# First embedding's projection ahead of and between the first attention's output projections, its input in tiles of the queries' kind

## The chip, the cores and the metric

One core of a Trainium2 chip runs the whole program. The metric is the device time of one execution in microseconds (us); the median of several runs is compared. TensorE (PE) multiplies, VectorE (DVE) and ScalarE (ACT) work on tiles, GpSimd (POOL) does part of that too, SyncE (SP) issues the DMAs.

## What is computed

A decoder of two layers over S = 256 tokens of width D = 1024. The first layer has differential attention (8 heads, each the difference of two softmaxes), the second latent attention; both go on with a gated feed-forward network and a per-layer embedding. Cut to what matters here:

```python
def diff_attention(h, pos, w_qkv, q_gain, k_gain, ...):
    q, k, v = ...                          # rms_norm(h @ w_qkv), per head
    a = softmax(causal(q @ k * scale + bias))
    wts = a[:, :, 0] - lam * a[:, :, 1]
    o = rms_norm(wts @ v, sub_gain) * (1.0 - lam_init)
    return o @ w_o

def per_layer_embedding(h, p_i, norm_g, w_proj, w_gate):
    gate = sigmoid(rms_norm(h, norm_g) @ w_gate)
    return (p_i @ w_proj) * gate

for i in range(2):
    h = h + attention_i(rms_norm(h, attn_norm[i]))
    h = h + conv_gated_ffn(rms_norm(h, ffn_norm[i]), ...)
    h = h + per_layer_embedding(h, p[i], ...)
```

The product `p_i @ w_proj` depends on no activation. It can be computed at any time before the embedding of its layer.

## The kernel before

Every float32 product is made of three faster ones: each operand is split into a high and a low part (`split`, L204 without and L205/L206 with a scale: ScalarE writes the high part, VectorE the difference), and `mm3` (L196 to L200) issues high x high, high x low and low x high into one PSUM tile. Activations lie transposed, features on the partitions.

Weights are streamed: `fetch` (L225) issues one DMA per unit of 128 x 1024 (512 KB) on SP's queue into a ring of five buffers (tile `st`), and `split_unit` has ScalarE cast it (L243, tile `wh`) and VectorE or POOL subtract (L244, tile `wl`), in turn by a share; there are four such pairs. The projection's two units of an embedding have a pair ring of their own (`xh`, `xl`), and their subtraction is always POOL's. A layout table (`_layout`, L1273) puts the units into memory in the order in which they are fetched.

In the first layer two streams of work are woven together (`weave`, L160). The main stream is the heads: `s1` makes a head's scores (tile `pb`; bias added at L554, exponentials at L558, reciprocals at L562/L563, and the combination of the two softmaxes, L565 on ScalarE and L566 on VectorE, tile `ex`); `s2` transposes that combination (tile `pc`) and splits it (`dr`); `s3` multiplies with the values (`pc`) and normalises (square L344, mean L350, a power on POOL L277, scaling L358, tile `da`); `s4` transposes the result and splits it with a gain into `og` (L205, L206). The filler stream `fl_a` (L737) gives the third and fourth projection of queries, keys and values, then the output projection `wo` of heads 0 to 3 and of heads 4 and 5 (tile `pa`, added to the residual at L632), and last the first embedding's input and projection: `pre_load` (L710) with `ple_p` (L703, DMA at L705, tile `d`, split at L204) and `pre_proj` (L717), four groups of twelve matmuls whose results ScalarE copies into `prj` (L732). `pre_proj` yields after each group. Behind the woven part come the output projection of heads 6 and 7, with the residual added in PSUM (L625) and split for the feed-forward (`hgH`, `hgL`), and the feed-forward itself.

A scheduler then sets each engine's order from these two streams and from tile rings: an engine works in that fixed order, and an instruction waits until all that it reads or overwrites is done. PSUM has rings `pa` (3), `pt` (1), `pb` (2) and `pc` (2). In SBUF, tiles of the kind `d` have 7 buffers, `dr` 4, `ex` 4 and `qk` (128 x 2 x 256, queries and keys) 22.

Of the kernel before, what the change touches and what calls it, by code (L numbers as in the profile page):

```python
# [10 lines left out]
F32R = mybir.dt.float32r  # L11
# [83 lines left out]
def trunk(ctx, tc, xT, xN, pT, pos, consts, grow, wall, out):  # L95
# [14 lines left out]
    def bankA():  # L110
        return bank("A")
# [16 lines left out]
    def d_tile(n=512, dt=F32):  # L128
        if dt == F32R:
            return tmp.tile([P, 512], F32R, tag="dr", name="dr", bufs=BUF_DR)[:, :n]  # L130
        return tmp.tile([P, 512], F32, tag="d", name="d", bufs=BUF_D)[:, :n]
# [10 lines left out]
    def f(ap):  # L142
        return ap.bitcast(F32)
# [8 lines left out]
    def later(lag, fn):  # L152
        late.append((clk[0] + lag, fn))
# [48 lines left out]
    def split(hi, lo, src, scale=None):  # L202
        if scale is None:
            return A.copy(hi, src).ins, V.tensor_sub(lo, src, f(hi)).ins  # L204
        return (A.activation(hi, src, AF.Copy, scale=scale).ins,  # L205
                V.scalar_tensor_tensor(lo, src, scale, f(hi), ALU.mult, ALU.subtract).ins)  # L206
# [26 lines left out]
    def ring_pair(tag="w", bufs=BUF_W):  # L233
        return tuple(ring.tile([P, UNIT], F32R, tag=tag + x, name=tag + x, bufs=bufs) for x in "hl")
# [12 lines left out]
    def load_unit():  # L247
        return split_unit(next(fetch()))
# [11 lines left out]
    def col(c, n=1):  # L260
        return cst[:, c:c + n]
# [24 lines left out]
    def qk():  # L286
        return act.tile([P, 2, S], F32R, tag="qk", name="qk", bufs=BUF_QK)
# [46 lines left out]
    def norm_block(ps, nb, width, eps, att=False):  # L334

        parts = [p[:, :nb * width] for p in ps] if isinstance(ps, list) else [ps[:, :NT * nb * width]]
        n, m = NT * nb * width, NT * nb
        s2 = a_tile() if att else d_tile(n)
        sg = "sa" if att else "s"
        ss = small(m, sg)  # L340
        z = n // len(parts)
        if width == P:
            for i in range(m):
                A.activation(s2[:, i * P:(i + 1) * P], ps[:, i * P:(i + 1) * P], AF.Square, accum_out=ss[:, i:i + 1])  # L344
        else:
            for i, p in enumerate(parts):
                A.activation(s2[:, i * z:(i + 1) * z], p, AF.Square)
            nbv[0] = V.tensor_reduce(ss, s2.rearrange("p (a b) -> p a b", b=width), AX.X, ALU.add).ins
        if isinstance(eps, float):
            V.tensor_scalar(ss, ss, 1.0 / width, eps, ALU.mult, ALU.add)  # L350
        else:
            V.scalar_tensor_tensor(ss, ss, 1.0 / width, eps[:, :m], ALU.mult, ALU.add)
        r = small(m, sg)
        rsqrt_(r, ss, m)
        dst = a_tile() if att else d_tile(n)
        w = m // len(parts)
        for i, p in enumerate(parts):
            nbv[1] = V.tensor_mul(dst[:, i * z:(i + 1) * z].rearrange("p (a b) -> p a b", b=width),  # L358
                                  p.rearrange("p (a b) -> p a b", b=width),
                                  r[:, i * w:(i + 1) * w].unsqueeze(2).to_broadcast([P, w, width])).ins  # L360
        return dst

    def to_T(src, dH, dL, gcol, bank=None):

        nb = src.shape[1] // (NT * P)
        pt = (bank or bankT)()
        for t in range(NT):
            for j in range(nb):
                i, o = t * nb + j, j * NT + t
                transpose(pt[:, o * P:(o + 1) * P], src[:, i * P:(i + 1) * P])  # L370
        split(dH.rearrange("p n x -> p (n x)"), dL.rearrange("p n x -> p (n x)"), pt[:, :NT * nb * P], gcol)
# [122 lines left out]
    def proj_a(p):  # L494
        todo = []

        def post(s, ps):
            dH, dL = qk(), qk()
            if s < 2:
                src = norm_block(ps, 4, 64, xs["eps"])  # L500
                if p == 1:
                    bst["after"] = bst.get("after", []) + nbv

                def fin():
                    to_T(src, dH, dL, gq[:, 0:1] if s == 0 else col(C_AK))
                    QA[p]["qk"[s]] = dH, dL
                later(LAG, fin)
            else:
                for t in range(NT):
                    split(dH[:, t], dL[:, t], ps[:, t * S:(t + 1) * S], xs["r"][:, t:t + 1])  # L510
                QA[p]["v"] = dH, dL

        for s in range(3):
            if p == 0 and s == 0:
                ps = first_block()
            else:
                ps = bankA()
                us = [(load_unit(), 4) for i in range(2)]
                block(8, us, S, 0, S, hgH, hgL, ps)
            yield 1  # L520
            todo.append((s, ps))
            if p == 0 and s == 0:
                epsx()
            elif p == 0 and s == 1:
                first_stats()
            elif p == 1 and s == 0:
                bias_prep()
            while "r" in xs and todo:
                post(*todo.pop(0))
# [122 lines left out]
    def wo(h0, kn, post=None):  # L652
        while not done.issuperset(range(h0, h0 + kn)):
            yield None
        yield from wst([(n, k) for n in range(NK) for k in range(kn)], lambda k: oH[(h0 + k) // 4][:, (h0 + k) % 4],
                       lambda k: oL[(h0 + k) // 4][:, (h0 + k) % 4], post)
# [15 lines left out]
    def first_block():  # L672
        ps = [bankA() for _ in range(NT)]
        for k, u, j in get_first():
            for t in range(NT):
                mm3(ps[t][:, :S], hgH[:, k, t * P:(t + 1) * P], hgL[:, k, t * P:(t + 1) * P],
                    u[0][:, j * S:(j + 1) * S], u[1][:, j * S:(j + 1) * S], k == 0, k == NK - 1)
        return ps

    def epsx():  # L680
        V.tensor_scalar(gq[:, 0:1], col(C_AQ), -SCALE_A, None, ALU.mult)
        V.tensor_scalar(gq[:, 1:2], col(C_QN), -SCALE_B, None, ALU.mult)
        V.tensor_scalar(gq[:, 2:3], col(C_ASUB), 1.0 - LAM_INIT, None, ALU.mult)
# [19 lines left out]
    def ple_p(l):  # L703
        pst = d_tile()
        nc.sync.dma_start(pst, pT[l].rearrange("p a b -> p (a b)"))  # L705
        pH, pL = d_tile(512, F32R), d_tile(512, F32R)
        split(pH, pL, pst)
        return pH.rearrange("p (a b) -> p a b", a=2), pL.rearrange("p (a b) -> p a b", a=2)

    def pre_load(l):  # L710

        share[0], was = 1.0, share[0]
        w = {"p": ple_p(l), "w": [split_unit(next(fetch()), ring_pair("x", 2)) for _ in range(2)]}
        share[0] = was
        return w

    def pre_proj(pjw):  # L717

        pH, pL = pjw["p"]
        us = pjw["w"]  # L720
        prj = pjw["y"] = act.tile([P, NK, S], F32, tag="prj", name="prj")
        for i in range(2):
            u = us[i]
            for j in range(2):
                ps = bankA()
                for m in range(2):
                    n = 2 * j + m
                    for k in range(2):
                        b = slice((2 * n + k) * P, (2 * n + k + 1) * P)
                        mm3(ps[:, m * S:(m + 1) * S], u[0][:, b], u[1][:, b], pH[:, k], pL[:, k], k == 0, k == 1)  # L730
                n = 4 * i + 2 * j
                A.copy(prj[:, n:n + 2].rearrange("p a b -> p (a b)"), ps)  # L732
                yield 1.3

    pj = []

    def fl_a():  # L737
        yield from proj_a(2)
        yield from proj_a(3)
        yield from wo(0, 4)  # L740
        yield from wo(4, 2)
        pj.append(pre_load(0))
        yield from pre_proj(pj[0])

    weave(chain(bias_mm(), attn_a()), fl_a(), RATIO_A)


# [484 lines left out]
def _layout(inp, np):  # L1232
    f = lambda n: np.asarray(inp[n], dtype=np.float32)
# [12 lines left out]
    def blocks(lst):  # L1246
        for a in range(0, len(lst), 8):
            units.append(np.concatenate(lst[a:a + 8], axis=1))

    def stationary(w, ks=None):  # L1250
        kt, nt = w.shape[0] // P, w.shape[1] // P
        ks = range(kt) if ks is None else ks
        return [w[k * P:(k + 1) * P, n * P:(n + 1) * P] for n in range(nt) for k in ks]
# [16 lines left out]
    for p in range(4):  # L1270
        for s in range(3):
            natural(wqkv[:, s * 1024 + p * 256:s * 1024 + (p + 1) * 256], 4)
    wo = f("a_w_o")[0]  # L1273
    for a, b in ((0, 4), (4, 6), (6, 8)):
        if a == 6:
            blocks(stationary(f("ple_w_proj")[0]))
        blocks(stationary(wo, range(a, b)))
    ffn(0)
    natural(f("w_dkv"), 3)
# [85 lines left out]
```

## Time and profile before

| | |
|---|---|
| median of 3 runs | 773.33 us (772.85 to 773.79) |
| the profiled execution | 773.53 us, its span 771.7 us |
| granted TensorE clock, mean | 0.998 |
| TensorE busy | 752.7 us, 98% of the span |
| VectorE busy | 571.9 us, 74% |
| ScalarE busy | 484.8 us, 63% |
| GpSimd busy | 257.0 us, 33% |

The span reaches from the first to the last instruction; the profiled execution's own time is 1.8 us longer. The granted clock is a share of TensorE's full speed. A busy time is the time in which at least one instruction of the engine runs; since matmuls overlap, the distance from one start to the next says what a matmul costs.

### The profile page before, as it was taken

How to read it: one execution, taken by the hardware profiler on the slowest of the kernel's cores; microseconds unless marked ns; L12 is line 12 of the kernel's file. 1: busy time of each engine (PE TensorE's matmuls, PEld its weight loads, DVE VectorE, ACT ScalarE, POOL GpSimd, SP SyncE). 2: the span in 40 equal slices, each digit the busy share in tenths (PEclk: the TensorE clock that was granted, in tenths of full speed). 3: DMA queues.
4: the chain of work that ended last, by engine and by line, in shares of the span. 5: the costliest groups of instructions: out<-in, count | busy, mean ns of one | idle time of the engine just before them, and what ended most of it. 6: DMA issues, size and time to landing. Idle time of an engine off the chain costs nothing.

```text
span 771.7 us, 16485 instructions
## 1 busy us (share of the span) xinstructions
PE 752.7 (98%) x6396; PEld 740.2 (96%) x6396; DVE 571.9 (74%) x1147; ACT 484.8 (63%) x1044; POOL 257.0 (33%) x181
## 2 busy tenths in 40 slices
PE   8999999999999999999999999999999999999996
PEld 7999988999999999999889999999999999999996
DVE  6677888668997795548688988776588778875445
ACT  6537777676666665447867876554676666655442
POOL 2664454233333411111414665131342332201230
PEclk9999999999999999999999999999999999999999
DMA  7994344255665576555355133334466566555531
GB/s 283 277 255 153 134 148 143 83 179 181 197 193 179 173 251 203 181 186 166 110 167 183 60 110 111 100 120 139 136 199 187 176 182 193 185 190 177 183 107 56
DMA packets 37519, 127.97 MB, mean 166 GB/s; under 512 B 4672, under 2 KB 6208, under 8 KB 37440
## 3 DMA queue, kind: packets, MB, share of 16 engines
q1 hardware_dynamic: 36432, 126.29, 52.3%
q8 instruction: 50, 0.82, 0.4%
q10 hardware_dynamic: 1008, 0.63, 0.3%
q14 instruction: 29, 0.24, 0.1%
HBM read 125.75 MB, written 1.15 MB: 164 GB/s over the span
## 4 chain that ended last, share of the span: by engine, by line
PE 86%; DVE 5%; ACT 5%; POOL 1%; issue 1%; DMA 1%; ACTq 0%; POOLq 0%
PE pa L198 18%; PE pa L200 18%; PE pa L199 18%; PE pc L200 8%; PE pc L199 8%; PE pc L198 8%; DVE wl L244 2%; ACT wh L243 1%; PE pt L192 1%; PE pb L198 1%; PE pb L199 1%; PE pc L192 1%; PE pb L479 1%; PE pb L200 1%; POOL wl L244 1%
## 5 line engine op out<-in xcount | busy, mean ns | idle before, releaser
L243 ACT CAST wh<-st 128x1024 fp32r<-128x1024 f32 x221 | 231.0, 1050 | 173.1 <-issue 67.9
L244 DVE TENSOR_TENSOR wl<-st,wh 128x1024 fp32r<-128x1024 f32 x166 | 210.8, 1271 | 105.2 <-ACT wh L243 104.9
L244 POOL TENSOR_TENSOR wl<-st,wh 128x1024 fp32r<-128x1024 f32 x55 | 134.8, 2451 | 208.7 <-ACT wh L243 200.2
L200 PE MATMUL pa<-hgH,wl 128*128 128x256 f32 x496 | 141.2, 285 | 0.4 <-POOL wl L244 0.4
L199 PE MATMUL pa<-hgL,wh 128*128 128x256 f32 x496 | 140.3, 283 | 0.0
L198 PE MATMUL pa<-hgH,wh 128*128 128x256 f32 x496 | 140.1, 283 | 0.0
L199 PE MATMUL pa<-og,wh 128*128 128x256 f32 x352 | 99.8, 284 | 0.9 <-DVE og L206 0.9
L301 POOL TENSOR_TENSOR ssq<-ssq,d 128x256 f32<-128x256 f32 x35 | 37.0, 1057 | 191.0 <-ACT d L300 169.3
L198 PE MATMUL pa<-og,wh 128*128 128x256 f32 x352 | 99.8, 286 | 0.3 <-ACT og L205 0.2
L200 PE MATMUL pa<-og,wl 128*128 128x256 f32 x352 | 99.7, 284 | 0.0
L200 PE MATMUL pc<-hgH,wl 128*128 128x256 f32 x336 | 95.4, 284 | 1.0 <-DVE wl L244 1.0
L200 PEld LDWEIGHTS pa<-hgH,wl 128*128 128x128 f32 x496 | 95.2, 192 | 0.7 <-POOL wl L244 0.6
L198 PE MATMUL pc<-hgH,wh 128*128 128x256 f32 x336 | 95.1, 284 | 0.4 <-DVE pa L793 0.4
L198 PEld LDWEIGHTS pa<-hgH,wh 128*128 128x128 f32 x496 | 95.1, 192 | 0.1
L199 PEld LDWEIGHTS pa<-hgL,wh 128*128 128x128 f32 x496 | 95.2, 192 | 0.0
L199 PE MATMUL pc<-hgL,wh 128*128 128x256 f32 x336 | 95.1, 283 | 0.1
L198 PE MATMUL pa<-wh,hgH 128*128 128x256 f32 x320 | 92.5, 294 | 1.5 <-ACT wh L243 0.8
L199 PE MATMUL pa<-wl,hgH 128*128 128x256 f32 x320 | 92.1, 289 | 1.2 <-DVE wl L244 0.6
L200 PE MATMUL pa<-wh,hgL 128*128 128x256 f32 x320 | 91.9, 288 | 0.3 <-DVE hgL L204 0.3
L199 PEld LDWEIGHTS pa<-og,wh 128*128 128x128 f32 x352 | 67.4, 191 | 1.2 <-DVE og L206 1.1
L198 PEld LDWEIGHTS pa<-og,wh 128*128 128x128 f32 x352 | 66.9, 191 | 1.1 <-ACT og L205 0.7
L200 PEld LDWEIGHTS pa<-og,wl 128*128 128x128 f32 x352 | 67.3, 191 | 0.1
(306 smaller groups left out, 1908.0 us busy)
## 6 DMA issues: line engine op xcount, KB each, us to landing
st<-in_wall SPq DMA_DIRECT2D x225, 512.0 KB, 3.6
oh<-s SPq DMA_DIRECT2D x24, 128.0 KB, 6.5
hT<-in_x SPq DMA_DIRECT2D x4, 256.0 KB, 4.9
st<-in_wall SPq DMA_DIRECT2D x4, 256.0 KB, 5.0
st<-in_xn SPq DMA_DIRECT2D x2, 512.0 KB, 7.2
d<-in_p SPq DMA_DIRECT2D x2, 256.0 KB, 3.8
out_h<-hT SPq DMA_DIRECT2D x4, 128.0 KB, 1.9
out_h<-hT ACTq DMA_DIRECT2D x4, 128.0 KB, 1.9
```

Of the source, the lines that this page charges most:

```text
L192: lastmm[0] = T.transpose(o, i, ident).ins
L198: T.matmul(ps, lhsT=aH, rhs=bH, start=start, stop=False)
L199: T.matmul(ps, lhsT=aH, rhs=bL, start=False, stop=False)
L200: lastmm[0] = T.matmul(ps, lhsT=aL, rhs=bH, start=False, stop=stop).ins
L243: A.copy(hi, st)
L244: eng.tensor_sub(lo, st, f(hi))
L301: sqlast[0] = G.tensor_add(sq, sq, t).ins
L479: T.matmul(ps[:, i * 32:(i + 1) * 32], lhsT=lh, rhs=tb[z], start=z == 0, stop=z == 2)
```

## The change

The two tiles of the embedding's input become tiles of the kind `qk` in place of `dr`, in both layers. In the first layer, `pre_load(0)` and the first two groups of the projection are put ahead of the output projection of heads 0 to 3, the other two groups between it and that of heads 4 and 5. The two weight units move ahead of all units of `wo` in the layout, and so in the order of the fetches.

```diff
--- before.py
+++ after.py
@@ -703,9 +703,9 @@
     def ple_p(l):
         pst = d_tile()
         nc.sync.dma_start(pst, pT[l].rearrange("p a b -> p (a b)"))
-        pH, pL = d_tile(512, F32R), d_tile(512, F32R)
-        split(pH, pL, pst)
-        return pH.rearrange("p (a b) -> p a b", a=2), pL.rearrange("p (a b) -> p a b", a=2)
+        pH, pL = qk(), qk()
+        split(pH.rearrange("p a b -> p (a b)"), pL.rearrange("p a b -> p (a b)"), pst)
+        return pH, pL
 
     def pre_load(l):
 
@@ -737,10 +737,13 @@
     def fl_a():
         yield from proj_a(2)
         yield from proj_a(3)
+        pj.append(pre_load(0))
+        ahead = pre_proj(pj[0])
+        yield next(ahead)
+        yield next(ahead)
         yield from wo(0, 4)
+        yield from ahead
         yield from wo(4, 2)
-        pj.append(pre_load(0))
-        yield from pre_proj(pj[0])
 
     weave(chain(bias_mm(), attn_a()), fl_a(), RATIO_A)
 
@@ -1271,9 +1274,8 @@
         for s in range(3):
             natural(wqkv[:, s * 1024 + p * 256:s * 1024 + (p + 1) * 256], 4)
     wo = f("a_w_o")[0]
+    blocks(stationary(f("ple_w_proj")[0]))
     for a, b in ((0, 4), (4, 6), (6, 8)):
-        if a == 6:
-            blocks(stationary(f("ple_w_proj")[0]))
         blocks(stationary(wo, range(a, b)))
     ffn(0)
     natural(f("w_dkv"), 3)
```

What the scheduler makes of it, at three places. The first is TensorE where the heads' stage gives way to the output projections: `pc` from `ex` are the transposes of head 5's combination, `pa` from `og` the output projection, `pa` from `qk` the embedding's projection. Before:

```order
L200 MATMUL pa_1934<-og_1461,wl_1917 128x256
L198 MATMUL pa_1920<-og_1461,wh_1916 128x256 [waits Activation_49]
L198 MATMUL pa_1934<-og_1461,wh_1916 128x256
L192 MATMUL pc_1882<-ident_103,ex_1708 128x128 [waits DVE_49,PE_49]
L192 MATMUL pc_1882<-ident_103,ex_1708 128x128 [waits DVE_49]
L192 MATMUL pc_1882<-ident_103,ex_1708 128x128
L199 MATMUL pa_1920<-og_1462,wh_1916 128x256 [waits DVE_49]
L546 MATMUL pb_1851<-qk_1764,qk_1620 128x128 [waits Activation_49]
L546 MATMUL pb_1852<-qk_1764,qk_1620 128x128 [waits PE_49]
```

The change:

```order
L199 MATMUL pc_1745<-qk_715,dr_1592 128x128
L200 MATMUL pc_1745<-qk_714,dr_1593 128x128
L192 MATMUL pc_1915<-ident_103,ex_1708 128x128 [waits DVE_49]
L198 MATMUL pa_1861<-qk_1844,xh_1850 128x256 [waits PE_49,Activation_49]
L198 MATMUL pa_1947<-qk_1844,xh_1850 128x256
L192 MATMUL pc_1915<-ident_103,ex_1708 128x128 [waits DVE_49]
L192 MATMUL pc_1915<-ident_103,ex_1708 128x128
L199 MATMUL pa_1861<-qk_1845,xh_1850 128x256 [waits DVE_49]
L200 MATMUL pa_1861<-qk_1844,xl_1851 128x256
```

The output projection of heads 0 to 3 left this place: its first matmuls stand behind the projection of `p` now, and the transposes come directly after the nine matmuls of a head's values (`pc` from `qk` and `dr`).

The second place is ScalarE just ahead of that, with the exponentials (L558) and the combination (L565) of head 5. Before:

```order
L558 ACTIVATE ex_1708,sa_1693<-ex_1708,sa_1692 128x128 [waits DVE_49,Activation_49]
L558 ACTIVATE ex_1708,sa_1693<-ex_1708,sa_1692 128x256 [waits DVE_49]
L558 ACTIVATE ex_1713,sa_1693<-ex_1713,sa_1692 128x128 [waits DVE_49]
L558 ACTIVATE ex_1713,sa_1693<-ex_1713,sa_1692 128x256 [waits DVE_49]
L204 CAST dr_1736<-pc_1732 128x384 [waits PE_49]
L565 ACTIVATE ex_1708<-ex_1708,sa_1718 128x128 [waits DVE_49]
L565 ACTIVATE ex_1708<-ex_1708,sa_1718 128x256 [waits Activation_49]
L243 CAST xh_2262<-st_2260 128x1024 [waits DMAHW4_49]
L243 CAST wh_2032<-st_2030 128x1024 [waits DMAHW0_49,PE_49]
L205 ACTIVATE qk_1836<-pa_1775,m_289 128x256 [waits PE_49]
L243 CAST wh_2098<-st_2096 128x1024 [waits DMAHW1_49]
L205 ACTIVATE og_1461<-pc_1740,gq_122 128x256 [waits PE_49]
```

The change:

```order
L558 ACTIVATE ex_1708,sa_1693<-ex_1708,sa_1692 128x128 [waits DVE_49,Activation_49]
L243 CAST wh_2111<-st_2109 128x1024 [waits DMAHW2_49,PE_49]
L558 ACTIVATE ex_1708,sa_1693<-ex_1708,sa_1692 128x256 [waits DVE_49]
L558 ACTIVATE ex_1713,sa_1693<-ex_1713,sa_1692 128x128 [waits DVE_49]
L558 ACTIVATE ex_1713,sa_1693<-ex_1713,sa_1692 128x256 [waits DVE_49]
L204 CAST dr_1736<-pc_1732 128x384 [waits PE_49]
L205 ACTIVATE qk_1836<-pa_1775,m_289 128x256 [waits PE_49]
L243 CAST wh_2169<-st_2167 128x1024 [waits DMAHW3_49]
L205 ACTIVATE og_1461<-pc_1740,gq_122 128x256 [waits PE_49]
L565 ACTIVATE ex_1708<-ex_1708,sa_1718 128x128 [waits DVE_49]
L565 ACTIVATE ex_1708<-ex_1708,sa_1718 128x256 [waits Activation_49]
L204 CAST qk_1844<-d_1842 128x512 [waits DMAHW7_49]
```

One weight cast stands between the exponentials now, the next between `qk` and `og`, and the combination behind both; the weight cast `xh` of the embedding went to an earlier place. POOL's subtraction for `wh_2169` follows two powers (L277) in its order, at the place where it had `xl_2263` and `wl_2099` before.

The third place is ScalarE where the last head's result is made, ahead of the feed-forward (`hgH`). Before:

```order
L243 CAST wh_2466<-st_2464 128x1024 [waits DMAHW2_49,PE_49,Pool_49]
L732 COPY prj_2272<-pa_2273 128x512 [waits DVE_49,PE_49,Activation_49]
L732 COPY prj_2272<-pa_2287 128x512 [waits PE_49]
L205 ACTIVATE og_2023<-pc_2211,gq_122 128x256 [waits PE_49]
L732 COPY prj_2272<-pa_2301 128x512 [waits PE_49]
L732 COPY prj_2272<-pa_2315 128x512 [waits PE_49]
L205 ACTIVATE hgH_2343<-pa_2335,cst_83 128x256 [waits DVE_49]
L205 ACTIVATE hgH_2343<-pa_2348,cst_83 128x256 [waits DVE_49]
```

The change:

```order
L344 ACTIVATE da_2211,sa_2212<-pc_2201 128x128 [waits DVE_49,PE_49,Pool_49]
L344 ACTIVATE da_2211,sa_2212<-pc_2201 128x128
L243 CAST wh_2466<-st_2464 128x1024 [waits DMAHW2_49,PE_49,Pool_49]
L205 ACTIVATE og_2036<-pc_2220,gq_122 128x256 [waits PE_49]
L205 ACTIVATE hgH_2343<-pa_2335,cst_83 128x256 [waits DVE_49,Activation_49]
L205 ACTIVATE hgH_2343<-pa_2348,cst_83 128x256 [waits DVE_49]
L205 ACTIVATE hgH_2343<-pa_2360,cst_83 128x256 [waits DVE_49]
```

The four copies of the projection's results (`prj`), which follow its 48 matmuls on TensorE, stood between the weight cast and `hgH`; they are gone from here. On VectorE the subtraction for `wh_2466` stands directly ahead of the lower half of the same `og` in both.

## Rows read from the trace of the kernel before

**Rows 1.** The page's first part: busy time by engine, share, instructions.

```profile
PE 752.7 (98%) x6396; PEld 740.2 (96%) x6396; DVE 571.9 (74%) x1147; ACT 484.8 (63%) x1044; POOL 257.0 (33%) x181
```

**Rows 2.** Windows: busy us (x instructions) per engine, granted clock, DMA share, GB/s.

```profile
80.00:100.00 20.00, 20.00 (x179) 19.02 (x178) 18.13 (x45) 16.25 (x47) 8.72 (x6) 1.00 0.33 109
100.00:120.00 20.00, 18.03 (x149) 16.56 (x149) 16.86 (x52) 15.73 (x49) 13.12 (x8) 1.00 0.48 159
...
160.00:340.00 180.00, 179.62 (x1500) 179.37 (x1499) 138.86 (x247) 111.45 (x182) 50.92 (x24) 1.00 0.63 196
```

**Rows 3.** Timeline of TensorE: start, duration, engine, line, instruction, [idle before <-releaser].

```profile
106.05 0.28 PE L198 MATMUL pa<-og,wh 128*128 128x256 f32 x1
...
109.03 0.28 PE L200 MATMUL pa<-og,wl 128*128 128x256 f32 x1
109.41 0.51 PE L198 MATMUL pa<-og,wh 128*128 128x256 f32 x2
109.76 0.49 PE L192 MATMUL pc<-ident,ex 128*128 128x128 f32 x3
111.14 0.39 PE L199 MATMUL pa<-og,wh 128*128 128x256 f32 x1 [0.89 <-DVE og L206]
...
116.88 0.62 PE L198 MATMUL pa<-og,wh 128*128 128x256 f32 x3 [0.16 <-ACT og L205]
...
118.10 0.28 PE L200 MATMUL pa<-og,wl 128*128 128x256 f32 x1
119.19 0.30 PE L192 MATMUL pc<-ident,ex 128*128 128x128 f32 x1 [0.82 <-DVE ex L566]
...
128.89 0.28 PE L200 MATMUL pa<-og,wl 128*128 128x256 f32 x1
129.82 0.41 PE L192 MATMUL pc<-ident,da 128*128 128x128 f32 x2 [0.66 <-DVE da L358]
```

**Rows 4.** Timeline of ScalarE, 102 to 108 us.

```profile
102.81 0.40 ACT L558 ACTIVATE ex<-ex,sa 128x128 f32<-128x128 f32 x1 [0.89 <-DVE sa L554]
...
105.70 1.03 ACT L243 CAST xh<-st 128x1024 fp32r<-128x1024 f32 x1
106.64 1.04 ACT L243 CAST wh<-st 128x1024 fp32r<-128x1024 f32 x1
```

**Rows 5.** Timeline of GpSimd, 99 to 104 us.

```profile
99.04 2.39 POOL L244 TENSOR_TENSOR wl<-st,wh 128x1024 fp32r<-128x1024 f32 x1 [2.90 <-ACT wh L243]
101.72 1.81 POOL L277 TENSOR_TENSOR s<-s,neghalf 128x8 f32<-128x8 f32 x1 [0.30 <-DVE s L352]
```

**Rows 6.** The page's DMA issues: count, KB each, median us to landing.

```profile
d<-in_p SPq DMA_DIRECT2D x2, 256.0 KB, 3.8
```

**Rows 7.** Timeline of VectorE, at 99, 102 and 118 us.

```profile
99.31 2.26 DVE L566 SCALAR_TENSOR_TENSOR ex<-ex,sa 128x128 f32<-128x128 f32 x1
...
102.36 0.15 DVE L350 TENSOR_SCALAR sa<-sa 128x2 f32<-128x2 f32 x1
...
118.70 0.35 DVE L566 SCALAR_TENSOR_TENSOR ex<-ex,sa 128x128 f32<-128x128 f32 x1
```

**Rows 8.** Timeline of ScalarE, at 141 us.

```profile
141.03 0.48 ACT L205 ACTIVATE og<-pc,gq 128x256 fp32r<-128x256 f32 x1
```

**Rows 9.** Timeline of VectorE, 138 to 145 us.

```profile
138.53 1.23 DVE L244 TENSOR_TENSOR wl<-st,wh 128x1024 fp32r<-128x1024 f32 x1 [0.25 <-ACT wh L243]
...
144.12 0.43 DVE L625 TENSOR_TENSOR pa<-pa,hT 128x256 f32<-128x256 f32 x1 [2.10 <-PE pa L200]
```

**Rows 10.** Timeline of TensorE, start of the feed-forward stage.

```profile
145.37 0.28 PE L198 MATMUL pc<-hgH,wh 128*128 128x256 f32 x1
145.72 0.39 PE L199 MATMUL pc<-hgL,wh 128*128 128x256 f32 x1
```

**Rows 11.** Timeline of TensorE, in the second layer's attention.

```profile
422.08 0.30 PE L198 MATMUL pb<-qk 128*128 128x128 f32 x1 [1.21 <-DVE s L350]
...
454.99 0.66 PE L192 MATMUL pt<-ident,d 128*128 128x128 f32 x4 [0.65 <-DVE qk L206]
```

## The prediction

> **What bounds the kernel now.** I read the page first: TensorE is busy 752.7 us of the 771.7 [rows 1], so time can only go or come in its gaps. Second, the busy time by window [rows 2]: 20.00 of 20 us at 80 to 100, 179.62 of 180 in the feed-forward stage at 160 to 340, where 1500 matmuls give a pitch of 0.12 us; but only 18.03 of 20 at 100 to 120. The attention heads' stage is where the loss is. Third, TensorE's timeline there [rows 3] names the waits, fourth the timelines of the engines that feed it. Where two rows of [rows 3] are apart by more than their matmuls need, I count the difference as lost. From 109.03 to 111.14 six matmuls (three of them transposes at 0.11) need 0.69 and take 2.11: 1.42 lost, most of it the wait of 0.89 for the second half of a normalised head (og, L206). From 118.10 to 119.19 0.97 is lost on the combination of two softmaxes (ex, L566), from 128.89 to 129.82 0.81, and 0.16 at 116.88. Together 3.4 us. The change can win no more than that here.
>
> **What moves and what doesn't.** The same 48 matmuls (5.8 us at pitch 0.12), two unit casts, two POOL splits, four prj copies and one p transfer are issued as before. The tiles of another kind add no instruction. Prices below come from rows; a step is a row's duration less about 0.1, since each ScalarE row begins that much before the one ahead ends (105.70 + 1.03 against 106.64 in [rows 4]).
>
> **Price 1, earlier weights and p: nothing.** The two projection units now come first of seven on SP's queue, and the other five two places later; their two splits take POOL some 14 us earlier, where TensorE has no gap at all (80 to 100, [rows 2]). Its cover is the matmuls of the fourth projection. Bounds: 0, and 2.4 us if one such split (2.39, [rows 5]) delayed a wait one to one. I take 0: carried into the new order, the split closest to the matmul that needs it still ends some 5 us ahead of it (an estimate). The p transfer stands behind the last of these units on SP and takes 3.8 us [rows 6]. Issued about 103, it lands by 107, while its cast stands on ScalarE behind work that ends at 109.7 (below). Not the bound.
>
> **Price 2, the first hole (about 107.6).** Before, nine matmuls of wo (the output projection) stood among the transposes here. Now TensorE reaches head 5's transposes (pc from ex) sooner: from 106.05 [rows 3] six transposes (0.57) and nine matmuls of 0.112 (1.0) bring it to 107.63. It then needs L566, and the way to it has grown. On ScalarE a weight cast (wh, 1.04) now stands between the first and second exp and waits for a matmul twelve matmuls and three transposes ahead of 106.05, which ends at about 104.55; then three exps, dr and qk (about 0.4 to 0.5 each, [rows 4]) end near 107.7, a second wh (1.04) ends near 108.7, and only then come og and L565, about 109.4. VectorE's L566 is ready at 109.5. But that second wh releases a POOL split at 108.8 that lasts 2.4.
>
> What such a split does is in the trace: L566 at 99.31 took 2.26 and ended with the POOL split of 99.04 + 2.39 = 101.43 [rows 5, 7]; the same instruction took 0.35 at 118.70. So L566 ends at about 111.3, and TensorE has waited 3.7. Two matmuls of the projection then run, and the third waits about 0.3 for p's lower half, whose VectorE step (0.7 as estimate, between 0.48 for 256 columns [rows 8, 9] and twice that) stands behind L566. New waits 4.0 against 3.4 gone: **+0.6**. Everything behind gains 4 us of lead in this stall and 24 matmuls of cover after it, so I let the waits of 119.19 and 129.82 vanish. Bounds: +2.4 if both stay (0.97 + 0.81), -0.5 if L566 isn't held.
>
> The Trainium skill, "SBUF — State Buffer", section "SBUF: two separate sides", says that the port pair shared by VectorE and GpSimd is an exclusive lock, held by whichever instruction started first for its whole length, and that a VectorE instruction with two SBUF inputs wants it against any GpSimd one that reads SBUF. For the splits the trace agrees (2.26 against 0.35 us); it is less clear for POOL's small powers, where L350, with one input, ran in 0.15 at 102.36 inside the 1.81 us power of 101.72 [rows 5, 7]. By the rule the sum is mine; were the lock not there it would be some 1.1 lower, the second rival below.
>
> **Price 3, the cover taken from the tail (137 to 146).** Before, the projection's 48 matmuls stood between the last two heads' output projections and the feed-forward, and head 7's chain (square, mean, power, scale, transpose, og twice) ran beneath them: only 0.23 us is lost, at 145.37 to 145.72 [rows 10]. Now nothing of it is left there. Counted from the end of head 7's values, 24 matmuls of wo cover 2.9 us, and the two transposes and three more matmuls bring TensorE to 3.5. og's upper half (0.48, [rows 8]) ends at 3.8: wait 0.4. Three matmuls later it needs og's lower half; on VectorE a weight split of 1.23 ([rows 9], 138.53), begun at 3.4, stands in front, so that half ends at 5.0: wait 0.85. Six matmuls, then the residual add (0.43), hgH (0.48) and hgL (0.48) follow one after the other with nothing between: waits of 0.7 and 0.45. Sum 2.4, less 0.23: **+2.1**. Bounds: +0.8 (only the three casts that follow each other) and +2.6 (the split begins later).
>
> **Price 4, the second layer: 0.** Its p tiles change ring too, and the order printed for 410 to 545 us shifts by some rows with the same work. The waits there that could go are 1.21 and 0.65 [rows 11]; the same size could come. Bounds -1.9 and +1.9, and I take 0, no row favouring either.
>
> **Sum.** 0.6 + 2.1 = +2.7 on the profiled execution's 773.53, so 776.2; the median of the runs shown, 773.33, is 0.2 lower: **776.0**. What this measurement can tell from no change is 0.2%, 1.55 us.
>
> **Rivals.**
> *Faster: head 5's combination isn't late.* If L566 is done before 107.6, TensorE finds p's projection without a wait and the hole is filled: -3.4 + 2.1 = -1.3, with one of the second layer's two waits gone -1.9 to -2.5: 771 to 772. For it: before, the exps began at 102.81 [rows 4], over 4 us ahead of the hole. Against: the wh now between the exps can't start before 104.55, a second one stands ahead of L565, and ScalarE works in its fixed order, so L565 can't pass them; TensorE would have to be some 2 us earlier at the matmul that frees the first, or 2 us later at the hole for reasons that cost nothing. Decides: L566's end against 107.6. Chance 0.15.
> *The split doesn't hold L566.* Should the POOL split come after L566 (its unit landing over 0.7 us late), L566 is done at 109.9; the wait is 2.3 and p's lower half costs 0.6: 2.9 - 3.4 + 2.1 = +1.6: 774.9, on the edge of same and slower. Against: in the order that fetch waits only for a split of the projections' weights, long done. Chance 0.15, half to each.
> *Given back later.* The second layer's new order loses its two waits: 776.0 - 1.9 = 774.1, no change to tell. For: 1.9 us of waits stand there. Against: nothing in the change aims at them. Chance 0.14.
>
> **How the numbers follow.** Forecast 0.56, its own range 775 to 778. Slower 0.56 + 0.07 = 0.63; same 0.14 + 0.08 = 0.22; faster 0.15. The range runs from 772.8, which leaves out most of the first rival, to 778.0, where the waits of 119.19 and 129.82 stay (776.0 + 1.8 = 777.8).
>
> **What would show it.** Right: in the profile after, one wait of 3 to 4 us near 107.6 on ex L566, an L566 of about 1.8 us that ends with a POOL split, no named wait of more than 0.3 us from 112 to 131, and near 140 three or four waits for og, hgH and hgL of 2 to 2.6 in sum, with 80 to 100 still full. Wrong: no wait at L566 (the first rival), a wait of 2.3 there (the second), waits below 1 us in the tail, or a difference of more than 1 us at 410 to 545. A wait for xl or for p's transfer would show price 1 wrong.

## The result, and the profile after

The change takes 778.17 us, median of 4 runs (776.34 to 778.48), against 773.2 before: a ratio of 1.0064, 95% interval 1.0051 to 1.0076. It is slower, as forecast, by 5.0 us where 2.7 were forecast, and 0.17 us outside the range.

The profiled execution of the change is the shortest of the four: 776.34 us, span 774.6, mean granted clock 0.994 in place of 0.998. Its busy times, the page's first part, answer to [rows 1]:

```profile
PE 753.2 (97%) x6396; PEld 740.8 (96%) x6396; DVE 569.1 (73%) x1147; ACT 485.8 (63%) x1044; POOL 258.4 (33%) x181
```

As much TensorE work as before, in a span that is 2.9 us longer. The windows answer to [rows 2]; the number behind POOL's busy time is the granted clock:

```profile
80.00:100.00 20.00, 20.00 (x178) 19.09 (x178) 16.78 (x45) 16.43 (x47) 13.32 (x8) 1.00 0.56 180
100.00:120.00 20.00, 16.13 (x126) 15.16 (x125) 14.89 (x41) 13.45 (x45) 7.04 (x5) 0.91 0.31 99
...
140.00:160.00 20.00, 17.99 (x131) 16.95 (x130) 13.25 (x28) 12.48 (x32) 4.71 (x7) 0.91 0.25 80
160.00:340.00 180.00, 179.69 (x1499) 179.43 (x1498) 138.75 (x247) 111.92 (x183) 51.90 (x25) 1.00 0.60 194
```

80 to 100 is still full (price 1). The two stretches of the forecast have lost work time, but both also show a clock of 0.91, which no part of the prediction had. TensorE's timeline around the first hole, to be read against [rows 3]:

```profile
106.64 0.28 PE L200 MATMUL pc<-qk,dr 128*128 128x128 f32 x1
110.78 0.47 PE L192 MATMUL pc<-ident,ex 128*128 128x128 f32 x1 [3.87 <-DVE ex L566]
...
112.37 0.42 PE L198 MATMUL pa<-qk,xh 128*128 128x256 f32 x1
112.59 0.41 PE L199 MATMUL pa<-qk,xh 128*128 128x256 f32 x1
...
114.03 0.28 PE L200 MATMUL pa<-qk,xl 128*128 128x256 f32 x1
```

TensorE waits 3.87 us for L566. Behind that, rows of 256 columns are some 0.21 apart (112.37 to 112.59) in place of 0.12, and only from 114.03 on as before. The clock by finer windows, at the hole and at the tail:

```profile
111.00:114.00 3.00, 3.00 (x15) 2.93 (x15) 2.64 (x7) 0.61 (x2) 0.70 (x1) 0.51 0.50 175
114.00:117.00 3.00, 3.00 (x29) 2.53 (x27) 0.15 (x1) 1.17 (x2) 0.00 (x0) 1.00 0.02 5
...
148.00:151.00 3.00, 2.90 (x12) 2.67 (x13) 1.35 (x4) 2.42 (x9) 1.24 (x2) 0.51 0.25 94
```

Where TensorE takes up work after either group of waits, the granted clock is at 0.5, the 1.2 GHz level, for some 3 us. The engines that feed the first hole, first GpSimd, then VectorE, then ScalarE ([rows 4, 5, 7] before):

```profile
108.23 2.35 POOL L244 TENSOR_TENSOR wl<-st,wh 128x1024 fp32r<-128x1024 f32 x1 [3.72 <-ACT wh L243]
```

```profile
108.51 0.48 DVE L206 SCALAR_TENSOR_TENSOR og<-pc,gq,og 128x256 fp32r<-128x256 f32 x1 [0.73 <-ACT og L205]
108.91 2.22 DVE L566 SCALAR_TENSOR_TENSOR ex<-ex,sa 128x128 f32<-128x128 f32 x2
```

```profile
103.62 0.40 ACT L558 ACTIVATE ex<-ex,sa 128x128 f32<-128x128 f32 x1 [1.01 <-DVE sa L554]
...
104.02 1.04 ACT L243 CAST wh<-st 128x1024 fp32r<-128x1024 f32 x1
...
107.06 1.04 ACT L243 CAST wh<-st 128x1024 fp32r<-128x1024 f32 x1
...
108.37 0.80 ACT L565 ACTIVATE ex<-ex,sa 128x128 f32<-128x128 f32 x2
```

It is the chain of price 2: a weight cast between the exponentials (104.02), a second one ahead of L565 (107.06), the POOL split that this releases (108.23, ending at 110.58), and two L566 that together take 2.22 us, which end at 111.13, 0.55 behind the split (rows with x2 stand for both). At the tail:

```profile
144.80 0.28 PE L200 MATMUL pa<-og,wl 128*128 128x256 f32 x1
145.29 0.62 PE L198 MATMUL pa<-og,wh 128*128 128x256 f32 x3 [0.21 <-ACT og L205]
146.51 0.39 PE L199 MATMUL pa<-og,wh 128*128 128x256 f32 x1 [0.60 <-DVE og L206]
...
147.20 0.28 PE L200 MATMUL pa<-og,wl 128*128 128x256 f32 x1
148.10 0.58 PE L198 MATMUL pc<-hgH,wh 128*128 128x256 f32 x1 [0.62 <-ACT hgH L205]
```

From start to start, less the matmuls between (one, three and one at 0.12), 0.37, 0.86 and 0.78 us are lost, for og's upper half, og's lower half and hgH. The next matmul, for hgL, starts 0.52 later, but already under the half clock. In the second layer, of the two waits of [rows 11] the first is still there and the second is gone (two of 0.31 and 0.27 at 393 went too, and one of 0.25 at 436 is new):

```profile
425.69 0.30 PE L198 MATMUL pb<-qk 128*128 128x128 f32 x1 [1.21 <-DVE s L350]
```

For the sums below I cut the time into three stages by the same four TensorE events in every profile: the matmul behind the last of the start's waits for a weight split (about 20 us), the first matmul of the first feed-forward (`pc` from `hgH`), the one (`pb` from `wh` and `og`, about 378) that waits 1.06 us for `og`, and the one of the second layer's end (`pc` from `hgH`, about 574) that waits 0.36 us for its residual. What lies before 20 us has the same order in all kernels but differs from run to run: that event is at 19.98 before, 18.92 in the first profile of the change and 19.79 in the second.

| profile | 20 us to first feed-forward | to 378 | to 574 |
|---|---|---|---|
| before | 125.4 | 232.6 | 195.9 |
| the change | 129.2 | 234.3 | 194.4 |
| the change, second profile | 130.3 | 234.5 | 194.4 |

First stage +3.8 to +4.9, second +1.7 to +1.9, third -1.6. Of the third, the waits just named make 1.0; no row names the rest.

### The profile page after: what moved, and what is told of

Read it like the earlier page. It is cut to its first block, busy times and chain, and to the rows that moved or that the text cites. A ratio compares the mean times of both kernels' runs of the same rounds, so it can differ in the third digit from the quotient of the medians.

```text
span 774.6 us, 16492 instructions
## 1 busy us (share of the span) xinstructions
PE 753.2 (97%) x6396; PEld 740.8 (96%) x6396; DVE 569.1 (73%) x1147; ACT 485.8 (63%) x1044; POOL 258.4 (33%) x181
## 4 chain that ended last, share of the span: by engine, by line
PE 89%; ACT 4%; DVE 4%; issue 1%; POOL 1%; DMA 1%; ACTq 0%; POOLq 0%
PE pa L198 19%; PE pa L199 19%; PE pa L200 19%; PE pc L200 8%; PE pc L199 8%; PE pc L198 8%; ACT wh L243 2%; DVE wl L244 1%; PE pt L192 1%; PE pc L192 1%; PE pb L198 1%; PE pb L199 1%; PE pb L200 1%; PE pb L546 1%; PE pb L479 1%
```

## Experiments

Each run's ratio is to the kernel before, on the same chip. `again`, `kind`, `half_late` and `p_early` stood side by side, then `p_early_half`, `flip`, `busy20` and `kind_qd`, then `busy36` and `place_dr`.

**The change again** (`again`), for a second profile.

> The changed kernel once more, for a second profile. Theory: it is 776.3 to 778.5 again, the wait for L566 in the first hole is 3.5 to 4.2 us, TensorE's granted clock is 0.50 for 3 to 4 us after that hole and again after the waits ahead of the feed-forward, and the first 25 us, whose order is the same as before, differ from the first profile of the change by the 1 us that was gained there by chance. Rival: the clock fall belongs to that one profile; then this one shows 1.00 after both places and is about 3.5 us shorter.

Measured 778.18 us (776.9 to 778.49), ratio 1.0065 (1.0052 to 1.0078). Its windows, behind the first hole and behind the tail's waits:

```profile
112.00:117.00 5.00, 5.00 (x25) 4.93 (x24) 2.53 (x7) 1.08 (x3) 0.70 (x1) 0.50 0.34 105
...
150.00:154.00 4.00, 3.82 (x19) 3.63 (x20) 1.73 (x5) 3.57 (x10) 1.46 (x2) 0.66 0.24 95
```

The wait is 3.87 us again, and both falls of the clock are there; the first is longer here, 0.50 over all of 112 to 117. The rival is out. Of the 1.1 us that the first profile was ahead at 20 us, 0.9 are gone; with the longer half clock that makes the 2.1 us between the two profiled spans (774.6 and 776.7). At the tail the clock fell later here, so the wait for hgL can be read at full clock:

```profile
150.04 0.38 PE L198 MATMUL pc<-hgH,wh 128*128 128x256 f32 x1 [0.62 <-ACT hgH L205]
150.56 0.38 PE L199 MATMUL pc<-hgL,wh 128*128 128x256 f32 x1
```

0.52 from start to start, less one matmul: 0.40 lost, against 0.23 before.

**The tile kind alone** (`kind`), nothing moved:

```diff
-        pH, pL = d_tile(512, F32R), d_tile(512, F32R)
-        split(pH, pL, pst)
-        return pH.rearrange("p (a b) -> p a b", a=2), pL.rearrange("p (a b) -> p a b", a=2)
+        pH, pL = qk(), qk()
+        split(pH.rearrange("p a b -> p (a b)"), pL.rearrange("p a b -> p (a b)"), pst)
+        return pH, pL
```

> The kernel before with only the tile kind changed (queries' kind for the embedding's input), nothing moved. Theory: the move makes the loss and the tile kind alone gives the second layer its new order, which in the profile of the change loses 1.5 us of waits between 380 and 550: 771.7, the heads' stage as before. Rival: the tile kind makes the loss (its ring or its order): 775 or more. Second rival: the second layer's gain comes from the move: 773.2.

Measured 778.02 us (776.43 to 781.23), ratio 1.0075 (1.0057 to 1.0094): as slow as the change, which I had not expected from any theory but the first rival. But the place is another one. Stages: 125.6, 232.6 and 199.9: all of it in the second layer, with waits on TensorE that neither the kernel before nor the change has:

```profile
437.94 0.38 PE L198 MATMUL pa<-wh,hgH 128*128 128x256 f32 x1 [0.67 <-DVE d L358]
...
440.91 0.63 PE L192 MATMUL pt<-ident,d 128*128 128x128 f32 x4 [1.26 <-DVE qk L206]
...
468.67 0.36 PE L198 MATMUL pa<-wh,hgH 128*128 128x256 f32 x1 [0.88 <-DVE d L358]
...
548.84 0.39 PE L198 MATMUL pc<-hgH,wh 128*128 128x256 f32 x1 [0.84 <-ACT wh L243]
```

In the first layer the clock fell here too, for some 3 us, although the waits up to there are those of the kernel before:

```profile
110.00:120.00 10.00, 8.96 (x62) 7.64 (x60) 8.03 (x30) 7.13 (x24) 6.30 (x4) 0.83 0.60 205
```

```profile
119.66 0.30 PE L192 MATMUL pc<-ident,ex 128*128 128x128 f32 x1 [0.15 <-DVE ex L566]
```

Yet the first stage is only 0.2 us longer than before. The waits behind the fall shrank: 0.15 for L566 in place of 0.82, and 0.27 for the scaling of `da` (L358) in place of 0.66. Slower matmuls ahead of a wait are hidden in it.

**The kind in the first layer's embedding only** (`kind_qd`):

```diff
+        if ('qk', 'dr')[l] == "qk":
+            pH, pL = qk(), qk()
+            split(pH.rearrange("p a b -> p (a b)"), pL.rearrange("p a b -> p (a b)"), pst)
+            return pH, pL
         pH, pL = d_tile(512, F32R), d_tile(512, F32R)
```

> The kernel before with the queries' tile kind for the first layer's embedding input alone; the second layer's has the old kind, nothing is moved. The order printed for the second layer is that of the run with the kind changed in both layers. Theory: what costs there is the order that the scheduler makes in the second layer, and that hangs on the first layer's use of the tile rings: 778 again, with waits of 5 to 7 us in sum between 410 and 560 against 2.6 before. Rival: the second layer's own tiles cost it (their ring is full there): 773.

Measured 776.57 us (775.94 to 776.96), ratio 1.0048 (1.0035 to 1.0062). Stages: 125.2, 232.6 and 199.9, with the same waits in the third. So it isn't the second layer's own tiles. What two tiles of the first layer take from one ring or the other changes the order that the scheduler makes 300 us later, and the stage takes 4 us more in that order. In the change, with the work moved as well, that stage has a third order, and takes 1.6 less than before.

**The last two groups put back** (`half_late`), so that the tail has 24 of its matmuls again:

```diff
         yield from wo(0, 4)
-        yield from ahead
         yield from wo(4, 2)
+        yield from ahead
```

> The change with the last two groups of the projection back behind the output projection of heads 4 and 5, ahead of that of heads 6 and 7. The first hole is the same by order. Theory: 24 matmuls (2.9 us) cover head 7's chain again, so the tail's waits (2 us) and the half clock behind them (1.7 us) go: 778.2 - 3.7 = 774.5, and only one fall of the clock is left, after the first hole. Rival: the half clock has another cause than the waits; then it stays and the time is about 776.2. Rival: the tail isn't where the time went: 778.

Measured 780.51 us (779.77 to 780.61), ratio 1.0097 (1.0083 to 1.011), a miss of 6 us in the total. The tail did what was expected; the second layer didn't stay:

```profile
148.64 0.38 PE L198 MATMUL pc<-hgH,wh 128*128 128x256 f32 x1 [0.62 <-ACT hgH L205]
...
471.19 0.35 PE L198 MATMUL pa<-wh,hgH 128*128 128x256 f32 x1 [1.47 <-DVE d L358]
```

Of the three waits only the one for hgH is left, and the stage behind it is back at 233.0: no half clock there. But the order of the second layer is a fourth one, with 199.2 in the third stage; in that stage the clock falls once more here, behind waits of 0.84 and 0.76 us at 551 and 552 (0.85 over 550 to 555), which left it at 1.00 in `kind`. I had read the order printed at the first hole, which was the same, and not the one behind it.

**The embedding's input fetched early** (`p_early`):

```diff
         yield from proj_a(2)
+        p0 = ple_p(0)
         yield from proj_a(3)
-        pj.append(pre_load(0))
+        pj.append(pre_load(0, p0))
```

`pre_load` then takes `p0` in place of its own call of `ple_p`.

> The change with the embedding's input fetched and split ahead of the fourth projection, so that the projection's matmuls wait for nothing near the first hole; the order then has 24 of them and 13 of the output projection ahead of head 5's transposes. Theory: the wait of 3.9 us for L566 goes, and with it the fall of the clock (1.7 us): 778.2 - 5.6 = 772.6 with the tail's loss still in. Rival: the wait for L566 only moves behind those matmuls, since a POOL split still holds it: 776 to 778. Rival: the wait goes and the clock falls nevertheless: 774.3.

Measured 772.27 us (770.72 to 773.78), ratio 0.999 (0.9981 to 0.9999). Stages: 124.9, 234.5, 194.4. TensorE's waits of more than 0.15 us from 20 to 150:

```profile
112.39 0.84 PE L546 MATMUL pb<-qk 64*128 64x128 f32 x10 [0.71 <-DVE qk L206]
...
142.18 0.62 PE L198 MATMUL pa<-og,wh 128*128 128x256 f32 x3 [0.56 <-ACT og L205]
143.03 0.39 PE L199 MATMUL pa<-og,wh 128*128 128x256 f32 x1 [0.23 <-DVE og L206]
...
144.63 0.39 PE L198 MATMUL pc<-hgH,wh 128*128 128x256 f32 x1 [0.62 <-ACT hgH L205]
```

The first hole is gone, with its half clock (1.00 from 100 to 140). The tail's waits are there, and the half clock behind them:

```profile
110.00:120.00 10.00, 9.29 (x80) 8.18 (x78) 7.19 (x23) 6.46 (x25) 1.83 (x2) 1.00 0.20 54
...
140.00:150.00 10.00, 8.44 (x52) 7.60 (x51) 5.83 (x14) 5.97 (x14) 2.01 (x3) 0.83 0.29 101
```

**Both together** (`p_early_half`): the input early and the last two groups back at the tail.

> The kernel with the embedding's input fetched ahead of the fourth projection, and with the last two groups of the projection put back behind the output projection of heads 4 and 5. Its order in the second layer is that of the change. Theory: the first hole stays filled, and the tail's waits (0.56, 0.23 and 0.62 in the profile without the last two groups' return) and the half clock behind them (1.7 us) go: 772.3 - 3.0 = 769.3. Rival: the tail's cover isn't what is missing there, the time stays at 772. Rival: as with the last two groups' return alone, the time gets longer.

Measured 770.45 us (769.92 to 771.41), ratio 0.9971 (0.9959 to 0.9982): faster than the kernel before, and by some 7 us than the change. Stages: 124.1, 233.0, 194.4. Against the kernel before that is -1.3, +0.5 and -1.6: most of what is won lies in the order of the second layer, at which the edit didn't aim, and the two stages that the move is about give 0.8. In the stretch of the four waits above, two are left, and the clock is 1.00 throughout:

```profile
112.43 0.84 PE L546 MATMUL pb<-qk 64*128 64x128 f32 x10 [0.71 <-DVE qk L206]
...
143.83 0.38 PE L198 MATMUL pc<-hgH,wh 128*128 128x256 f32 x1 [0.62 <-ACT hgH L205]
```

```profile
140.00:150.00 10.00, 8.68 (x66) 7.91 (x66) 5.92 (x14) 6.55 (x17) 1.82 (x3) 1.00 0.23 60
```

**No POOL split at the hole** (`flip`):

```diff
         yield next(ahead)
+        turn[0] = (turn[0] + 0.5) % 1.0
         yield from wo(0, 4)
+        turn[0] = (turn[0] + 0.5) % 1.0
```

> The change with the turn of the output projection's first four weight splits swapped, so that the one behind the second cast is VectorE's and none of POOL's starts at the first hole; the second layer's order is the change's. Theory of the lock: L566 takes 0.35 to 0.5 us in place of 1.8 or more. The next thing late is p's cast, which stands behind L565 on ScalarE, so TensorE still waits 2.5 to 3.3 us in place of 3.9, and the clock falls all the same: 777 to 778. Rival: the lock is the whole of the hole: a wait below 1 us, no fall of the clock, 773. Rival: no lock: L566 as long as in the change, 778.

Measured 778.11 us (777.47 to 779.34), ratio 1.0072 (1.0059 to 1.0085). VectorE and TensorE at the hole:

```profile
108.84 1.23 DVE L244 TENSOR_TENSOR wl<-st,wh 128x1024 fp32r<-128x1024 f32 x1 [0.45 <-ACT wh L243]
...
110.38 0.74 DVE L566 SCALAR_TENSOR_TENSOR ex<-ex,sa 128x128 f32<-128x128 f32 x2
```

```profile
110.43 0.51 PE L198 MATMUL pa<-qk,xh 128*128 128x256 f32 x2 [2.76 <-ACT qk L204]
...
111.77 0.39 PE L199 MATMUL pa<-qk,xh 128*128 128x256 f32 x1 [0.16 <-DVE qk L204]
```

Without a split on POOL the two L566 take 0.74 us together, in place of 2.22. The wait is 2.76 now and ends with the cast of the embedding's input on ScalarE (qk L204), and the clock falls behind it all the same (0.50 at 113 to 115). The Trainium skill's lock ("SBUF — State Buffer", section "SBUF: two separate sides") agrees with both numbers. It is real, but this run doesn't show what the hole would be without it: the split that POOL gave up is now VectorE's, and its 1.23 us stand ahead of L566. From the last matmul ahead of the hole to the third of the projection 3.7 us are lost (2.9 and 0.8 from start to start), in place of 4.0. What both kernels share is ScalarE's part: its L565 ends some 2.4 us behind the start of the hole and p's cast some 2.9, so that much of the hole doesn't hang on the lock.

The equal total says less than it seems to. The stages are 128.8, 234.5 and 195.3: the first is 0.4 to 1.4 shorter than in the two profiles of the change, and the third 0.9 longer, with a wait of 0.69 for hgL at 399 that the change doesn't have, though the expectation had taken the order there to be the same.

**Useless matmuls ahead of the hole** (`busy20`, `busy36`), on the change:

```diff
                 ps = bankA()
+                if pjw is pj[0] and not (i or j):
+                    for _ in range(20):
+                        T.matmul(ps[:, :S], lhsT=us[0][0][:, :P], rhs=us[0][0][:, :S], start=True, stop=True)
```

> The change with 20 useless matmuls (2.4 us at pitch 0.12) written into the projection's PSUM tile just ahead of the first hole; nothing reads their result. Theory of the clock: the wait shrinks to 1.0 to 1.8 us, the granted clock stays 1.00 at 105 to 125, and the first matmul of the feed-forward comes 2 to 3 us earlier than in the change, though there are 20 matmuls more. Rival: the half clock there has another cause, or costs nothing: the feed-forward starts at the time of the change or up to 2.4 us later. The second layer's order is another one here, so the total says little and the stage up to 150 us is read.

Measured 778.96 us (778.09 to 779.86), ratio 1.008 (1.0066 to 1.0095). The expectation failed. Two waits were left, the second for p's lower half, which VectorE makes behind L566, and the clock fell behind it:

```profile
110.24 0.51 PE L198 MATMUL pa<-qk,xh 128*128 128x256 f32 x2 [0.24 <-ACT qk L204]
112.67 0.58 PE L199 MATMUL pa<-qk,xh 128*128 128x256 f32 x1 [1.93 <-DVE qk L204]
```

```profile
110.00:120.00 10.00, 7.83 (x39) 7.20 (x39) 5.12 (x9) 3.55 (x11) 2.17 (x2) 0.66 0.22 60
```

The granted clock over 110 to 120 is 0.66 here, 0.83 in the first profile of the change and 0.66 in the second: no shorter a fall than there. The feed-forward began 131.3 us after the event at 20 us, 1.1 to 2.2 later than in the change. The tail's three waits (0.21, 0.61, 0.62) are as in the change, and left the clock at 1.00. With 36:

> The change with 36 useless matmuls (4.3 us) ahead of the first hole in place of 20, which left waits of 2.2 us and the clock at half; nothing reads their result. The second layer's order is the change's, so totals compare. Theory of the clock: the wait of 3.9 us is filled with work, the granted clock stays 1.00 at 105 to 125, and 36 matmuls more cost nothing or give 0.5 to 2.5 us back: 776 to 778. Rival: the half clock costs nothing that the waits don't: the matmuls take the place of the wait and the time stays 778.2 with the clock at 1.00. Rival: waits remain or the clock falls nevertheless: 779 or more.

Measured 775.97 us (774.54 to 776.98), ratio 1.0033 (1.0021 to 1.0045). Stages: 128.6, 233.0, 194.4.

```profile
112.18 0.39 PE L199 MATMUL pa<-qk,xh 128*128 128x256 f32 x1 [0.53 <-DVE qk L204]
```

```profile
110.00:120.00 10.00, 9.47 (x82) 8.79 (x82) 6.22 (x18) 5.45 (x20) 1.68 (x2) 1.00 0.20 54
...
140.00:150.00 10.00, 8.44 (x64) 7.62 (x64) 7.41 (x16) 5.50 (x17) 1.27 (x2) 1.00 0.35 107
```

4.3 us of work that nothing reads make the change 2.2 us faster. They stand where TensorE waited and cost nothing there: the projection's third matmul comes 92.9 us after the event at 20 us, with them as without. What comes back is the half clock. Not all of it is the first hole's: the tail's waits are as in the change, but the clock didn't fall behind them in this profile. Against the two profiles of the change the first stage is 0.6 to 1.7 us shorter, and the second, behind the tail, 1.2 to 1.4. All twelve runs (774.54 to 776.98) lie below 777, six of the change's eight above 778.

**The new place with the old tile kind** (`place_dr`): the diff of the change without its first part.

> The change's new place for the projection with the old tile kind. The order printed for the second layer is that of the run in which the last two groups went back, which has 1.5 to 3 us more of waits there than the change. Theory: the loss in the first layer stays, since the place makes it, and the second layer adds 2 to 4 us: 780 to 782. Rival: the tile kind makes the loss of the change: 773 to 775.

Measured 784.69 us (784.19 to 786.3), ratio 1.0149 (1.0123 to 1.0176). Stages: 132.4, 233.0, 199.6. The wait at the hole is 3.96, and the clock stays at half for nearly all of 110 to 120. Together the stages are 11 us above the kernel before, more than the 780 to 782 of the expectation:

```profile
110.00:120.00 10.00, 7.98 (x37) 6.86 (x38) 6.77 (x20) 4.95 (x18) 2.42 (x2) 0.51 0.22 73
```

The place makes the loss in the first layer, with either tile kind. It is 2.2 to 3.2 us larger here than in the change; part of that is the longer half clock, whose length differs between two profiles of one kernel too, so that the tile kind kept the loss lower isn't shown. In the second layer the kind goes with the better order (194.4 against 199.6, which again has a fall of the clock in it, 0.67 over 555 to 560).

## Why the prediction was wrong

By its own steps:

- *Price 1, nothing:* right. No wait for xl or for p's transfer, 80 to 100 full.
- *Price 2, waits of 4.0 at the hole:* right in place, cause and size. From 106.64 to 110.78 TensorE lost 4.0 (forecast 3.7 and 0.3), L566 was held to the end of the POOL split, and no named wait of over 0.15 stood between 112 and 131. How much of the hole is the lock stays open: the second rival (a wait of 2.3, then 0.6) had L566 free of any split, and `flip`, the nearest run, lost 2.9 and 0.8 with VectorE's own split ahead of it. Its time, 774.9, lacked the half clock as my own did.
- *Price 3, 2.4 in the tail:* right. 0.37 + 0.86 + 0.78 = 2.0 against my 0.4, 0.85 and 0.7, and for hgL 0.40 against 0.45, read in the second profile, where the clock was still full.
- *Price 4, 0 for the second layer:* -1.6 in the change, within the bounds, but by luck. The same work in other orders came out at 194.4 to 199.9 us, 1.6 below the kernel before to 4.0 above it. "No row favouring either" was true; that the range is bounded by the waits that were there was not.
- *The sum: the step that failed.* It took a wait to cost its own length. The rows show a second term behind each: TensorE at half its clock after it. At the hole TensorE worked at half from 110.8 to 114.0 in the first profile and from 111.7 to 117.1 in the second. Of each 0.21 us between rows some 0.09 is lost there, so that makes 1.4 us of the 3.2 and 2.3 of the 5.4, an estimate that the first stage bears out: less the waits, 1.2 and 2.3 us of its growth are left. Behind the tail it cost 1.2 and 1.4: the second stage takes 234.25 and 234.45 with the fall, and 233.04 at most in the five runs whose clock stayed full there behind the wait for hgH (`half_late`, `p_early_half`, `busy20`, `busy36`, `place_dr`). The Trainium skill, "TensorE: Matmul & The Clock Gate", section "Part 1: The HAM clock gate", has TensorE go to 1.2 GHz after it was idle. The rows at 0.50 agree. The kernel before kept 1.00 over 100 to 120 through its own waits [rows 2], and the prediction has no term for the clock.

For the second profile, of a run at 778.49: waits 4.0 - 3.4 at the hole and 2.4 - 0.2 in the tail are +2.8, half clock 2.3 + 1.4 = +3.7, a wait for a weight split in the feed-forward (0.50 in place of 0.20) +0.3, second layer -1.6, start -0.2: +5.0, and the span grew from 771.7 to 776.7, by 5.0. The waits' part is the prediction's +2.7 almost to the tenth, and two terms were left out that partly cancel, +3.7 and -1.6. The sign was safe; the size was not.

What stays open: why the clock falls behind some waits and not others. The same 0.89 for og at 111 left it at 1.00 in the kernel before and took it to 0.83 (mean of 110 to 120) in the run with the tile kind alone; the tail's three waits halved it in both profiles of the change and not with 20 or 36 useless matmuls. That this chance makes part of the spread of the runs is a guess; the mean granted clocks of the change's runs lie between 0.990 and 0.995.

## What to carry to other kernels

Price a wait on TensorE twice: its length, and what the clock may take behind it, 1.2 to 2.3 us here behind waits of 2 to 4 us; filling such a wait even with useless work can pay. The second price is lost only where nothing later waits anyway: in `kind` a fall of 3 us cost the stage 0.2. Work that is moved to fill a hole must have its own inputs ready there: with the small input fetched one projection earlier, and half of the work left where it was to cover the other hole, the move gave -2.1 us in place of +5.0, of which 0.8 in the two stages it touches. Where a scheduler sets the order, two tiles in another ring can reorder a stage 300 us later; over all edits here that stage came out at -1.6 to +4.0 us: compare the order of every stage, not only of the edited one, before a difference is put down to the edit.

## What the runs showed that I had not expected

A change of ring for two or four small tiles, with nothing moved, cost 0.48 and 0.75%; the whole change cost 0.64%. More matmuls made a kernel faster (775.97 against 778.18 us). And the half clock did not get shorter with the wait: TensorE worked at it for 3.2 and 5.4 us behind 3.87 us in the two profiles of the change, and for 5.8 us behind 1.93 in `busy20`, so that shortening the wait without closing it brought nothing there.
